# The begin of the second MLP product: three steps put in another order

## The chip, the cores and the metric

The kernel runs on one core of a Trainium2 chip. TensorE (PE in the profile) multiplies, VectorE (DVE), ScalarE (ACT) and GpSimd (POOL) work on elements, and SyncE (SP) issues the transfers between the chip's memory and the core. Each engine has a queue of its own and takes its instructions in the order in which the program gave them; engines wait for each other through semaphores. The metric is the device time of one execution in microseconds (us), lower is better.

## The reference

The kernel computes one layer of an encoder on 1024 tokens of width 1024, in float32. The part that matters here is the last line, the MLP:

```python
h = rms_norm(x, norm2_g[l]) @ w_mlp_in[l]          # 1024 x 4096
x = x + jnp.square(jax.nn.relu(h)) @ w_mlp_out[l]  # 4096 x 1024
```

Before it come a combined input projection, neighbourhood attention, a short gated convolution and the merge of both branches.

## The kernel before

Every float32 operand is scaled by a power of two and split into two float16 parts, a high part (written by ScalarE, `A.activation`) and a low part (the rest, written by VectorE, `V.scalar_tensor_tensor`). A product is three matmuls: high by high, high by low, low by high (`PASSES`).

Both MLP products save multiplications by working on 2 x 2 blocks with seven products in place of eight. Sums of blocks take the place of the eighth product.

*First MLP product.* It runs in 16 groups of columns (`quad(q)`, L1284). A group has seven banks of twelve matmuls. The first bank's result is copied by ScalarE (L1307); the others are added by VectorE straight out of PSUM into the group's tile `as` (the sums `post5`, `post7`, `post3` and two lambdas, L1295 to L1310). When a group's last sum is given out, a generator `h_done(q)` (L1267) is started. It makes relu on ScalarE (L1269), the square with its row sums (L1271), then four sums of blocks on POOL (`sums`, L1134, its instructions at L1138), and then one store of all seven forms to the chip's memory (`HS`, L1275).

*Second MLP product.* It runs over four slices `s` of the 4096, and in each over seven operands, in the order of `ORDER` (L1345): w11, t2, w21, t3, t1, t4, w22. An operand holds one form of h and one form of the weights, each with high and low part (tile `ops`). TensorE takes four banks of twelve matmuls for an operand (loop at L1479). `prep2(s)` (L1347) prepares the operands of a slice:

- it squares the weights on ScalarE (L1362, L1365) and has VectorE add the squares up (L924, L925). A small matmul (L179, on TensorE's own queue) sums over the partitions, and VectorE makes the slice's scale of that;
- POOL makes the weight form T2 (L1371, L1372);
- then for each operand it asks for the h of a later one (`h_load(n + 3)`, L1343, on SP's queue), lets ScalarE write the high part of h (L1397), VectorE the low part of h (L1399), ScalarE the high part of the weights in two halves (L1402) and VectorE the low part in two halves (L1406);
- behind some operands POOL makes the next weight forms in place: after w11 it adds w12 to w11 (L1411, two adds of 128 x 1024), after t2 it adds w22 to w12 (L1415), after t3 it completes T2 (L1419).

Operand 1 (t2 of slice 0) has a peculiarity: its h was loaded into the place where its weights' high part will be (L1377, L1378), so ScalarE's L1402 waits for VectorE's L1399.

*The order.* Nothing schedules itself. The program is written by generators: `fg` holds those that end the work of a group, `bg` those that prepare what comes. `unit` (L185) gives out the matmuls of a bank and then takes some steps of `fg` (`step`) and `bg` (`tick`). So the place of a `yield` decides where an instruction stands in its engine's queue. `need(i)` (L1182) ticks and steps until operand `i` has been given out in full; `gate(i)` keeps a generator back until TensorE's work that used the same place has been given out (`pe_done`). After group 15 the program loads the h of operands 2, 3 and 4, calls `settle()`, which gives out the sums that wait for their bank, and steps until no group is alive:

```python
    settle()
    while live:
        step()
```

Seen queue by queue, the kernel before has, around the change: VectorE has operand 0's low parts, operand 1's low parts, and among and behind these the last five sums of group 15. ScalarE has operand 0's and operand 1's high parts, then group 15's relu. POOL has group 14's four sums, the four adds L1411 and L1415, and then group 15's four sums. SP has group 14's store, the h of operands 2, 3 and 4, then group 15's store, the h of operands 5, 6 and 7, and the weights of slice 1.

Of the kernel before, what the change touches and what calls it, by code (L numbers as in the profile page):

```python
# [15 lines left out]
OP = mybir.AluOpType  # L16
# [36 lines left out]
def encoder_block(ctx: ExitStack, tc: tile.TileContext, x, weights, cols, gqk, rel, masks, out):  # L53
    nc = tc.nc
    V, A, G, T, SP = nc.vector, nc.scalar, nc.gpsimd, nc.tensor, nc.sync
# [27 lines left out]
    def cols_of(kind, n):  # L83
        a = area[kind]
        if a[1] + n > a[2]:
            assert kind != "keep"
            a[1] = a[0]
        a[1] += n
        return slice(a[1] - n, a[1])

    def keep(n=1):
        return cols_of("keep", n)
# [4 lines left out]
    def at(c, i, n=1):  # L97
        return slice(c.start + i, c.start + i + n)

    def mul(a, b, out=None):  # L100
        out = out or tmp(a.stop - a.start)
        V.tensor_tensor(sc[:, out], sc[:, a], sc[:, b], op=OP.mult)
        return out
# [23 lines left out]
    def step(n=1):  # L127
        for _ in range(n):
            for g in list(fg):
                if not advance(g):  # L130
                    fg.remove(g)

    def tick(n=1):

        for _ in range(n):
            i = 0
            while i < len(bg):
                r = advance(bg[i])
                if not r:
                    bg.pop(i)  # L140
                elif r == WAIT and side[0]:
                    i += 1
                else:
                    break
# [55 lines left out]
    def settle():  # L200
        while late:
            late.pop(0)()
# [9 lines left out]
    def load_upto(n):  # L212
        while loaded[0] < min(n, len(loads)):
            ch, p = loads[loaded[0]]
            loaded[0] += 1
            t = rawp.tile([128, 1024], F32, name="raw")
            load_into(t[:, :ch.widths[p][0] * ch.widths[p][1]], ch, p)
            ch.raw.append(t)
# [702 lines left out]
    def sum_of(sm):  # L921

        b, a = cols_of("prep", 1), ones_col()
        V.tensor_reduce(sc[:, b], sc[:, sm], axis=AX, op=OP.add)  # L924
        V.tensor_copy(a, sc[:, b])  # L925
        return a, work[0]

    def scale_of(am, more, n=3):

        a, mark = am  # L930
        yield from apart(mark, n * 6144, work)
        b, s, inv = cols_of("prep", 1), cols_of("prep", 1), keep()
        yield from all_sum(a, b, anybank(), 1e-36)
        yield from pow2_half(b, 14, s, inv, more)
        return s, inv
# [238 lines left out]
    pe_done, ready = [-2], set()  # L1174
# [3 lines left out]
    def gate(i):  # L1178
        while pe_done[0] < i - 2 or (i == 2 and pair_done[0] < 4):
            yield  # L1180

    def need(i):  # L1182
        while i not in ready:
            assert bg
            forced[0] = True
            tick()
            step()
        forced[0] = False
# [145 lines left out]
    def w2x_load(s):  # L1334
        pool = later["pool"] if s == 1 else wsp
        X2[s] = pool.tile([128, 4, 1024], F32, name="w2x", tag="w2x" if s == 1 else "ws", bufs=1 if s == 1 else 2)
        for i in range(4):
            load_into(X2[s][:, i], c2x[s], i)

    def h_load(n):  # L1340
        s, f = n // 7, ORDER[n % 7][0]
        later["h", n] = later["hf"][:, n % 4]
        SP.dma_start(later["h", n], HS[s][:, f])  # L1343
# [3 lines left out]
    def prep2(s):  # L1347
        raw, x2 = c2[s].raw, X2[s]
        w11, w12 = raw[0:2], raw[2:4]
        w21, w22 = [x2[:, i] for i in range(2)], [x2[:, i] for i in range(2, 4)]  # L1350
        while not r_ready[s]:
            yield
        Rs, iR = R[s]
        sm = cols_of("prep", 6)
        if s == 0:
            yield from gate(16)
            OPS[16] = TAGS[16 % 3][0].tile([128, 2, 2, 2048], F16, name="ops", tag=TAGS[16 % 3][1])
            j = OPS[16][:, 0, 0].bitcast(BF16)
        else:
            j = later["junk"]  # L1360
        for i in range(4):
            A.activation(j[:, :1024], raw[i], AF.Square, scale=sc[:, iR], accum_out=sc[:, at(sm, i)])  # L1362
            yield
        for i in range(2):
            A.activation(j, x2[:, 2 * i:2 * i + 2].rearrange("p a c -> p (a c)"), AF.Square, scale=sc[:, iR],  # L1365
                         accum_out=sc[:, at(sm, 4 + i)])
            yield
        sums = sum_of(sm)
        T2 = later["t2"]()
        for i in range(2):  # L1370
            G.tensor_tensor(T2[:, i], w12[i], w22[i], op=OP.add)  # L1371
            G.tensor_tensor(T2[:, i], T2[:, i], w11[i], op=OP.add)  # L1372
        yield
        if s == 0:
            yield from gate(17)
            P = OPS[17] = TAGS[17 % 3][0].tile([128, 2, 2, 2048], F16, name="ops", tag=TAGS[17 % 3][1])
            later["h", 1] = P[:, 0].rearrange("p w m -> p (w m)").bitcast(F32).rearrange("p (k t) -> p k t", k=4)  # L1377
            SP.dma_start(later["h", 1], HS[0][:, ORDER[1][0]])  # L1378
        sw, inv = yield from scale_of(sums, 0)
        fw = keep()  # L1380
        mul(iR, sw, fw)
        c2[s].inv = inv
        yield
        for o, (f, name) in enumerate(ORDER):
            n = 7 * s + o
            i = 16 + n
            yield from gate(i)
            pool, tag = TAGS[i % 3]
            if n > 1:
                OPS[i] = pool.tile([128, 2, 2, 2048], F16, name="ops", tag=tag)  # L1390
            P = OPS[i]
            while ("h", n) not in later:
                yield
            if 1 < n < 25:
                h_load(n + 3)
            hf = later.pop(("h", n)).rearrange("p k t -> p (k t)")
            A.activation(P[:, 1, 0], hf, AF.Copy, scale=sc[:, Rs])  # L1397
            yield
            V.scalar_tensor_tensor(P[:, 1, 1], hf, sc[:, Rs], P[:, 1, 0], op0=OP.mult, op1=OP.subtract)  # L1399
            w = {"w11": w11, "t1": w11, "t3": w12, "w21": w21, "w22": w22}.get(name) or [T2[:, i] for i in range(2)]  # L1400
            for i2 in range(2):
                A.activation(P[:, 0, 0, 1024 * i2:1024 * i2 + 1024], w[i2], AF.Copy, scale=sc[:, fw])  # L1402
            yield
            for i2 in range(2):
                sl = slice(1024 * i2, 1024 * i2 + 1024)
                V.scalar_tensor_tensor(P[:, 0, 1, sl], w[i2], sc[:, fw], P[:, 0, 0, sl], op0=OP.mult, op1=OP.subtract)  # L1406
                yield
            ready.add(i)
            if name == "w11":
                for i2 in range(2):  # L1410
                    G.tensor_tensor(w11[i2], w11[i2], w12[i2], op=OP.add)  # L1411
                yield
            elif name == "t2":
                for i2 in range(2):
                    G.tensor_tensor(w12[i2], w12[i2], w22[i2], op=OP.add)  # L1415
                yield
            elif name == "t3":
                for i2 in range(2):
                    G.tensor_tensor(T2[:, i2], T2[:, i2], w21[i2], op=OP.add)  # L1419
                yield  # L1420
            elif name == "t1":
                done[0] += 4
                load_upto(done[0] + 5)
                if s < 3:
                    w2x_load(s + 1)
                    bg.append(prep2(s + 1))
            yield
# [8 lines left out]

    bg.append(first2())
    bg.append(prep2(0))
    whole(14)
    whole(15)  # L1440
# [3 lines left out]
    for n in (2, 3, 4):  # L1444
        h_load(n)
    settle()
    while live:
        step()
    p4.close()
# [3 lines left out]
    t2 = w5p.tile([128, 2, 1024], F32, name="t2")  # L1453
# [119 lines left out]
```

## Time and profile before

| | |
|---|---|
| median of 3 runs | 1279.17 us (1278.58 to 1280.23) |
| the profiled execution | 1279.16 us, its span 1277.0 us |
| mean granted clock of TensorE | 0.985 |
| busy: TensorE, its weight loads | 1214.9 us (95%), 578.5 us (45%) |
| busy: VectorE, ScalarE, POOL | 961.3 us (75%), 763.7 us (60%), 463.0 us (36%) |
| share of TensorE in the chain that ended last | 66% |
| second MLP product | from 975.5 us to the end |

A row of a timeline reads: start, duration, engine, line of the kernel, operation, output tile and input tiles, shapes, how many instructions it merges, and in brackets how long the engine stood idle before it and what ended that. Times are us from the span's start. Matmul ends are modelled: one of 512 columns shows 0.379 us, while the next starts 0.216 us after it at full clock. The row of a tile gives the least, the median and the largest duration in ns, then the first and last start.

### The profile page before, as it was taken

To read this page: it belongs to the slowest core of one execution; us is meant where nothing else is said; L and a number is where in the kernel's file an instruction comes from. 1 tells how busy PE (TensorE), PEld (TensorE's weight loads), DVE (VectorE), ACT (ScalarE), POOL (GpSimd) and SP (SyncE) were. 2 spreads that over 40 slices of the span, in tenths; PEclk is the share of its full clock that TensorE was granted. 3 is DMA by queue.
4 is the path that set the end of the run, shared out by engine and by line. 5 is a ranking of instruction groups with operands and counts; after the bars stand their busy time and mean duration, and the time that the engine had idled before them with its cause. 6 is when DMAs were issued, how large, how long until landed. Compare 5 with 4: busy or idle time off the path is not lost.

```text
span 1277.0 us, 17035 instructions
## 1 busy us (share of the span) xinstructions
PE 1214.9 (95%) x6294; PEld 578.5 (45%) x6294; DVE 961.3 (75%) x1719; ACT 763.7 (60%) x1169; POOL 463.0 (36%) x277
## 2 busy tenths in 40 slices
PE   4999998998999999999997999999998999999998
PEld 3544444444444444444445644444443444444444
DVE  6668767878656876876576467766767889999997
ACT  6777567677564544533575777787774873646440
POOL 2430001211222111100112467866669455463462
PEclk9999998999999999999998999999999999999999
DMA  6558446556543212215277344534457553526212
GB/s 250 115 195 178 86 85 132 105 106 134 116 112 100 66 34 66 60 40 198 66 150 146 115 162 178 176 129 157 173 205 264 217 203 132 198 100 247 95 37 99
DMA packets 170803, 173.35 MB, mean 136 GB/s; under 512 B 131424, under 2 KB 131936, under 8 KB 166624
## 3 DMA queue, kind: packets, MB, share of 16 engines
q1 hardware_dynamic: 170720, 172.27, 45.5%
q8 instruction: 49, 0.80, 0.3%
q14 instruction: 34, 0.28, 0.1%
HBM read 102.51 MB, written 37.75 MB: 110 GB/s over the span
## 4 chain that ended last, share of the span: by engine, by line
PE 66%; DVE 15%; ACT 8%; DMA 5%; issue 4%; POOL 2%; SPq 1%; DVEq 0%; ACTq 0%; POOLq 0%
PE ps_d L188 24%; PE ps_s L188 22%; PE ps_o L188 14%; PE ps_d L854 5%; DMA PT<-P 2%; DMA hs<-as 2%; DVE w_s L971 1%; DVE w_ws L278 1%; ACT w L977 1%; POOL sform L480 1%; PE ps_s L778 1%; PE ps_o L835 1%; DVE sz L792 1%; DVE sc L301 1%; ACT raw L944 1%
## 5 line engine op out<-in xcount | busy, mean ns | idle before, releaser
L188 PEld LDWEIGHTS <-w 128*128 128x128 f16 x1512 | 148.2, 99 | 161.3 <-issue 11.0
L188 PEld LDWEIGHTS <-ops 128*128 128x128 f16 x1356 | 133.1, 98 | 164.1 <-issue 8.5
L1138 POOL TENSOR_TENSOR as<-as 128x512 f32<-128x512 f32 x64 | 110.8, 1731 | 69.0 <-ACT as L1271 65.3
L854 PE MATMUL ps_d<-uT,w_ws 128*128 128x512 f16 x528 | 129.7, 387 | 2.5 <-ACT w_ws L290 2.4
L188 PE MATMUL ps_d<-ops 128*128 128x512 f16 x492 | 115.4, 385 | 4.3 <-DVE as L1298 4.3
L188 PE MATMUL ps_s<-ops 128*128 128x512 f16 (+1 forms) x528 | 118.7, 375 | 0.0
L1397 ACT ACTIVATE ops<-hf,sc 128x2048 f16<-128x2048 f32 x26 | 52.0, 1999 | 95.1 <-PE ps_d L188 39.9
L188 PEld LDWEIGHTS <-uT 128*128 128x128 f16 x648 | 64.7, 100 | 70.5 <-issue 6.7
L971 DVE SCALAR_TENSOR_TENSOR w<-raw,sc,w 128x512 f16<-128x512 f32 (+1 forms) x32 | 40.7, 1271 | 67.8 <-ACT w L977 67.8
L188 PE MATMUL ps_d<-u2T,w 128*128 128x512 f16 (+1 forms) x420 | 89.0, 363 | 1.9 <-DMA u2T<-v 1.9
L188 PEld LDWEIGHTS <-w_s 128*128 128x128 f16 x588 | 57.1, 98 | 73.2 <-DMA uT<-gs 2.9
L188 PE MATMUL ps_s<-u2x,w 128*128 128x512 f16 (+1 forms) x396 | 83.3, 360 | 4.2 <-ACT v L1163 2.1
L944 ACT ACTIVATE raw<-raw,sc 128x256 f32<-128x256 f32 x184 | 76.0, 495 | 6.7 <-DVE w_ws L278 3.4
L958 POOL TENSOR_TENSOR tsum<-raw 128x512 f32<-128x512 f32 x30 | 50.8, 1707 | 79.7 <-ACT raw L944 66.5
L854 PEld LDWEIGHTS <-w_ws 128*128 128x128 f16 x528 | 51.6, 99 | 59.7 <-issue 5.6
L1399 DVE SCALAR_TENSOR_TENSOR ops<-hf,sc,ops 128x2048 f16<-128x2048 f32 x26 | 72.3, 2781 | 7.3 <-ACT ops L1397 7.3
L188 PE MATMUL ps_o<-ops 128*128 128x512 f16 x336 | 77.1, 379 | 0.0
L1269 ACT ACTIVATE as<-as 128x2048 f32<-128x2048 f32 x16 | 30.6, 1910 | 65.2 <-DVE as L1303 65.2
L958 POOL TENSOR_TENSOR gsum<-raw 128x512 f32<-128x512 f32 x14 | 18.5, 1340 | 135.6 <-issue 68.6
L971 DVE SCALAR_TENSOR_TENSOR w<-tsum,sc,w 128x1024 f16<-128x1024 f32 x30 | 61.5, 2088 | 0.0
L278 DVE SCALAR_TENSOR_TENSOR w_ws<-raw,sc,w_ws 128x512 f16<-128x512 f32 (+2 forms) x72 | 51.1, 764 | 3.5 <-ACT w_ws L290 3.5
L290 ACT ACTIVATE w_ws<-raw,sc 128x512 f16<-128x512 f32 (+2 forms) x72 | 40.9, 636 | 20.0 <-DVE sc L253 20.0
(302 smaller groups left out, 2558.5 us busy)
## 6 DMA issues: line engine op xcount, KB each, us to landing
raw<-in_weights SPq DMA_DIRECT2D x92, 512.0 KB, 4.1
hs<-as SPq DMA_DIRECT2D x16, 1792.0 KB, 6.9
hf<-hs SPq DMA_DIRECT2D x26, 1024.0 KB, 6.3
w2x<-in_weights SPq DMA_DIRECT2D x16, 512.0 KB, 7.4
raw<-in_weights SPq DMA_DIRECT2D x16, 384.0 KB, 3.8
xt<-in_x SPq DMA_DIRECT2D x8, 512.0 KB, 9.9
gs<-s SPq DMA_DIRECT2D x4, 1024.0 KB, 7.0
x<-in_x SPq DMA_DIRECT2D x8, 512.0 KB, 8.3
```

Source lines behind the costliest of these rows:

```text
L188: T.matmul(ps, l, r, start=a, stop=b)
L278: V.scalar_tensor_tensor(lo, self.raw[p][:, o:o + m], sc[:, c:c + 1], hi, op0=OP.mult, op1=OP.subtract)
L290: A.activation(self.parts[:, 0, f + o:f + o + m], self.raw[p][:, o:o + m], AF.Copy, scale=sc[:, c:c + 1])
L301: V.tensor_reduce(sc[:, at(rm, o, k)], self.raw[p][:, :k * w].rearrange("p (k w) -> p k w", k=k), axis=AX, op=OP.max, apply_absolute_value ...
L854: T.matmul(ps, l, r, start=a, stop=b)
L944: A.activation(v, v, AF.Copy, scale=sc[:, at(g, 4 * i + k)])
L958: G.tensor_tensor(t[:, o], a, b, op=OP.add)
L971: V.scalar_tensor_tensor(P[:, a:b, 1], w, sc[:, s], P[:, a:b, 0], op0=OP.mult, op1=OP.subtract)
L1138: sub.tensor_tensor(z[o], z[a], z[b], op=op)
L1269: A.activation(f[:, 0:4], f[:, 0:4], AF.Relu)
L1397: A.activation(P[:, 1, 0], hf, AF.Copy, scale=sc[:, Rs])
L1399: V.scalar_tensor_tensor(P[:, 1, 1], hf, sc[:, Rs], P[:, 1, 0], op0=OP.mult, op1=OP.subtract)
```

## The change

```diff
@@ prep2, for each operand n
             A.activation(P[:, 1, 0], hf, AF.Copy, scale=sc[:, Rs])
             yield
+            while n == 1 and pe_done[0] < 16:
+                yield
             V.scalar_tensor_tensor(P[:, 1, 1], hf, sc[:, Rs], P[:, 1, 0], op0=OP.mult, op1=OP.subtract)
...
             ready.add(i)
-            if name == "w11":
-                for i2 in range(2):
-                    G.tensor_tensor(w11[i2], w11[i2], w12[i2], op=OP.add)
-                yield
-            elif name == "t2":
-                for i2 in range(2):
-                    G.tensor_tensor(w12[i2], w12[i2], w22[i2], op=OP.add)
+            if name == "t2":
+                for a, b in ((w11, w12), (w12, w22)):
+                    for i2 in range(2):
+                        G.tensor_tensor(a[i2], a[i2], b[i2], op=OP.add)
                 yield
...
@@ after whole(15) and the loads of operands 2, 3 and 4
     settle()
+    need(17)
     while live:
         step()
```

It has three parts. The generator that prepares operand 1 stops ahead of the low part of h (L1399 before, L1401 after) until all matmuls of group 15 have been given out. The two adds to w11 move from behind operand 0 to behind operand 1, in front of the two adds to w12; this holds for all four slices. And after `settle()` the program gives out the rest of operand 1 before it steps on.

The number of instructions on every engine stays the same. In the built program the queues of slice 0 become: VectorE has operand 0's low parts, the last five sums of group 15, then operand 1's low parts, then operand 2's. ScalarE keeps its order. POOL has group 14's four sums, the first sum of group 15, the four adds, and then the other three sums of group 15. SP keeps its order. TensorE keeps its order.

## The prediction

> **What bounds the kernel now.** I read four views in this order: the busy times by stretch, TensorE's timeline where the first MLP product gives way to the second, the timelines of the other engines there, and the transfers behind. By stretch:
>
> ```profile
> 975.50:1277.00 301.50, 293.44 (x1360) 133.29 (x1358) 277.66 (x248) 145.91 (x131) 153.88 (x52) 0.99 0.43 157
> ```
>
> The columns are the stretch, its length, then the busy us of TensorE, its weight loads, VectorE, ScalarE and POOL, then the granted clock. The second product is TensorE's: 293.44 of 301.50 us. What is missing lies at its begin (twelve matmuls fill one bank):
>
> ```profile
> 975.49 2.75 PE L188 MATMUL ps_o<-ops 128*128 128x512 f16 x12
> 978.08 2.75 PE L188 MATMUL ps_d<-ops 128*128 128x512 f16 x12
> 980.67 2.75 PE L188 MATMUL ps_s<-ops 128*128 128x512 f16 x12
> 987.75 5.28 PE L188 MATMUL ps_d<-ops 128*128 128x512 f16 x12 [4.32 <-DVE as L1298]
> 992.82 3.21 PE L188 MATMUL ps_s<-ops 128*128 128x512 f16 x12
> 995.87 2.75 PE L188 MATMUL ps_o<-ops 128*128 128x512 f16 x12
> ```
>
> Banks follow each other every 2.59 us (975.49, 978.08, 980.67). Operand 0's fourth bank should start at 983.26 and starts at 987.75; it and a part of the next run slowly. The bank of 995.87 would have stood at 975.49 + 5 × 2.59 = 988.44, so the whole loss is 7.43 us. That is all this place can give. The slow part is the clock (stretch, length, TensorE's busy us, granted clock):
>
> ```profile
> 983.42:987.75 4.33, 0.01 (x2) 0.90 1.00 416
> 987.75:993.90 6.15, 6.15 (x15) 0.51 0.17 71
> ...
> 733.50:737.90 4.40, 1.65 (x8) 0.98 0.94 324
> 737.90:741.20 3.30, 3.29 (x9) 0.51 0.68 265
> ```
>
> After an idle stretch of 4.33 us TensorE is granted 0.51 of its clock for 6.15 us; after one of 2.75 us (4.40 − 1.65) for 3.30 us. Half the clock loses half of that: 1.65 to 3.1 us.
>
> VectorE holds the bank up:
>
> ```profile
> 970.41 2.34 DVE L1399 SCALAR_TENSOR_TENSOR ops<-h,sc,ops 128x2048 f16<-128x2048 f32 x1
> ...
> 976.09 4.43 DVE L1399 SCALAR_TENSOR_TENSOR ops<-ops,sc 128x2048 f16<-128x2048 f32 x1
> 981.79 2.02 DVE L1406 SCALAR_TENSOR_TENSOR ops<-h,sc,ops 128x1024 f16<-128x1024 f32 x1 [1.28 <-ACT ops L1402]
> ...
> 984.34 2.76 DVE L1406 SCALAR_TENSOR_TENSOR ops<-h,sc,ops 128x1024 f16<-128x1024 f32 x1
> 987.02 0.68 DVE L1298 TENSOR_TENSOR as<-ps_d,as 128x512 f32<-128x512 f32 x1
> ...
> 988.93 0.68 DVE L1303 TENSOR_TENSOR as<-ps_s,as 128x512 f32<-128x512 f32 x1
> ```
>
> ```profile
> 975.05 7.68 POOL L1411 TENSOR_TENSOR raw<-raw 128x1024 f32<-128x1024 f32 x2 [1.17 <-DVE ops L1406]
> ```
>
> ```profile
> L1371 POOL TENSOR_TENSOR h<-raw,w2x x2: 2352/2360/2367, 956.1 to 960.9; 128x1024 f32<-128x1024 f32 x2
> ```
>
> ```profile
> L1138 POOL TENSOR_TENSOR as<-as x64: 1261/1600/3331, 715.4 to 999.7; 128x512 f32<-128x512 f32 x64
> ```
>
> ```profile
> L1406 DVE SCALAR_TENSOR_TENSOR ops<-raw,sc,ops x24: 1271/1273/3378, 972.7 to 1236.0; 128x1024 f16<-128x1024 f32 x24
> ```
>
> Group 15's sums (L1298 to L1303) stand behind operand 1's low parts. These are slow because POOL runs: 4.43 us beside it against 2.34 without, the halves 2.02 and 2.76 against 1.27; and two of POOL's adds take 7.68 us where one takes 2.36 alone (a sum of a group, L1138, at least 1.26). 4.43 is 2.34 and the rest of an add: the two engines take turns, an instruction at a time. Sums out of PSUM keep their 0.68.
>
> **The change part by part.** No instruction is added or removed; the order alone changes.
>
> *Sums ahead of operand 1's low parts.* VectorE has done operand 0's halves at 976.1. Five sums, 0.6 to 0.7 apart (L1310, L1298 to L1303), end at 979.2, and the one that frees the bank (L1300) at 978.7, before 983.26. The wait and its clock drop go: 7.43 us. TensorE now wants operand 1 at 975.49 + 4 × 2.59 = 985.85.
>
> *The adds leave POOL.* From 974 on POOL is idle, so operand 1's low part of h takes 2.34 (979.2 to 981.5). ScalarE's high parts of its weights wait for that, as before:
>
> ```profile
> 980.61 2.19 ACT L1402 ACTIVATE ops<-h,sc 128x1024 f16<-128x1024 f32 x2 [6.01 <-DVE ops L1399]
> 989.65 1.91 ACT L1269 ACTIVATE as<-as 128x2048 f32<-128x2048 f32 x1 [6.85 <-DVE as L1303]
> ...
> 993.50 0.19 ACT L1271 ACTIVATION_READ_ACCUMULATOR as<-as,sc 128x1 f32 x1
> ```
>
> They run from 981.6 to 983.8, and with two halves at 1.27 operand 1 is complete at 985.3, in time by half a microsecond; a miss costs TensorE that much.
>
> *Relu behind operand 1.* It starts at 983.8 instead of 989.65 and ends, as the row of 993.50 does 4.04 after it, at 987.8. ScalarE's high part of operand 2's h then ends at 989.7.
>
> *What POOL does next.* In the built order POOL has group 15's first sum, the four adds, the other three sums and the store. That first sum waits for the relu, and the adds behind it: they start at 989.1, just ahead of operand 2's low parts at 989.7. With the lengths alone, less a tenth that neighbours overlap (2.3 an add, 1.2 a sum, 2.2 and 1.1 VectorE's 2048 and 1024 columns), the turns are: add to 991.4, operand 2's low h 993.6, add 995.8, first half 996.9, add 999.1, second half 1000.2, add 1002.4, operand 3's low h 1004.6, sum 1005.8, half 1006.9, sum 1008.0, half 1009.1, sum 1010.3. TensorE wants operand 2 at 985.85 + 10.36 = 996.2. Its second matmul waits for the first half (0.5), its eighth for the second (2.0): 2.6 us, for now. Operand 2 ends at 1009.1, when operand 3 is ready.
>
> *What is late next.* Group 15's store goes at 1010.3 instead of 1001.90, and on SP's queue stand behind it the h of operands 5, 6 and 7 and the next weights:
>
> ```profile
> 1001.90 0.53 SPq L1275 DMA_DIRECT2D hs<-as  x1
> 1002.48 5.20 SPq L1343 DMA_DIRECT2D hf<-hs  x3
> ```
>
> ```profile
> L1343 SPq DMA_DIRECT2D hf<-hs x1: 654/654/654, 1002.5 to 1002.5; - x1
> ...
> DMA to landing us min/median/max: 10.6/10.6/10.6
> ```
>
> ```profile
> 997.56 0.67 ACT L1493 ACTIVATE acc<-ps_o,sc 128x512 f32<-128x512 f32 x1
> 998.13 0.67 ACT L1493 ACTIVATE acc<-ps_d,sc 128x512 f32<-128x512 f32 x1
> ...
> 1014.20 2.00 ACT L1397 ACTIVATE ops<-hf,sc 128x2048 f16<-128x2048 f32 x1 [4.01 <-PE ps_d L188]
> 1016.11 2.17 ACT L1402 ACTIVATE ops<-h,sc 128x1024 f16<-128x1024 f32 x2
> 1018.19 0.67 ACT L1493 ACTIVATE acc<-ps_s,sc 128x512 f32<-128x512 f32 x1
> ...
> 1025.14 1.99 ACT L1397 ACTIVATE ops<-hf,sc 128x2048 f16<-128x2048 f32 x1
> ```
>
> ```profile
> 1038.87 0.16 DVE L925 CAST ones<-sc 128x1 bf16<-128x1 f32 x1
> ```
>
> ```profile
> 1039.89 0.17 PE L179 MATMUL ps_d<-ones 128*128 128x1 bf16 x1
> ```
>
> Operand 5's h landed at 1002.48 + 10.6 = 1013.1, and ScalarE took it at 1014.20: 1.1 us of slack. Now it lands at 1010.3 + 0.6 + 10.6 = 1021.5. Behind the waiting L1397 stand, in ScalarE's order, operand 5's weights, four evictions (L1493), operand 6, and all the squares of the next weights (L1362, L1365). VectorE adds these up (L925), and TensorE's own queue holds the small matmul L179 on that sum. L179 came 0.86 us after its input: no room there either.
>
> From operand 5's h to that input: 4.0 us to the first eviction (1014.20 to 1018.19), 2.3 for four at 0.57 apart (997.56, 998.13), then 1025.14 to 1039.03, 13.9: together 20.2. It is ready at 1021.5 + 20.2 = 1041.7. TensorE gets there at 1039.89 − 7.43 + 2.6 = 1035.1, or 1035.4 with a short wait for VectorE's eviction of operand 2's first bank. It waits 6.3 us, and L179 runs at 1041.7, 1.8 us later than before. Whatever was won or lost earlier drops out.
>
> A wait of 6.3 us is longer than the two above, so the clock drops again: 1.65 to 3.1 us. I take the middle, 2.4; the two rows show both lengths and nothing says which.
>
> The Trainium skill ("TensorE: Matmul & The Clock Gate", "The HAM clock gate") says the clock halves after an idle window of about 3.4 us and returns after a busy one, with windows that run free. By it, one to two windows at half clock cost 1.7 to 3.4 us and the sum would be 1282.7 to 1284.4 (an estimate); the rows' 3.30 and 6.15 us agree.
>
> Behind L179 operand 7 needs some 12 us on VectorE and ScalarE, and TensorE has six banks (15.5 us) until then: nothing more is lost.
>
> **Sum.** The profiled execution took 1279.16 us (span 1277.0); the median is 1279.17. 1279.16 + 1.8 + 2.4 = 1283.4. With the store a microsecond off either way (about one turn) this case alone holds 1281.6 to 1285.1.
>
> **The rivals.** *Faster: the store is not late.* If POOL's eight instructions ran at their length alone from 987.8, the store would go at 987.8 + 4 × 1.3 + 4 × 2.36 = 1002.4, operand 5's h land at 1013.6, L179's input be ready at 1033.8, before TensorE: 1279.16 − 7.43 + 2.9 = 1274.6. It decides for a store before about 1006: L179 would be 31.4 later, at 1037.4, and a drop of 2.4 bring it back to 1039.9. For it: POOL is idle until 987.8. Against it: the 7.68 for two adds, with six of VectorE's low parts in the same stretch.
>
> The Trainium skill ("SBUF — State Buffer", "Who interferes with whom") makes it a lock: a VectorE instruction with two SBUF inputs and a GpSimd one that reads SBUF exclude each other for a whole instruction. The rows of 4.43 and 0.68 agree, and by it the sum stays 1283.4.
>
> *No measurable change.* The store goes at 1008.5, L179 falls where it was, and the drop is the small one: 1279.16 + 1.65 = 1280.8. Or the change doesn't do what it says: the stall goes from the bank to operand 2's low parts, with L179 in time, and two drops leave 1279.16 − 7.43 + 2.9 + 2 × 2.4 = 1279.4. For it: terms of a few microseconds that nearly cancel. Against it: 1.8 us of turns would have to go.
>
> *Slower still.* The store takes longer, as an earlier one did (13.5 us against 8.9 for that of 1001.90):
>
> ```profile
> L1275 SPq DMA_DIRECT2D hs<-as x1: 525/525/525, 953.2 to 953.2; - x1
> ...
> DMA to landing us min/median/max: 8.0/10.8/13.5
> ```
>
> ```profile
> L1275 SPq DMA_DIRECT2D hs<-as x1: 525/525/525, 1001.9 to 1001.9; - x1
> ...
> DMA to landing us min/median/max: 8.9/8.9/8.9
> ```
>
> That is 4.6 us more for operand 5's h: 1288.0. Against it: the queue is empty at 1010, as at 1001.90.
>
> **How the numbers follow.** Forecast 0.68, slower still 0.05, no measurable change 0.14, faster 0.13. So slower by over 0.2% (2.6 us, about what a measurement here can tell) 0.73, within it 0.14, faster 0.13. The range leaves out the faster case and the worst: 1277.5 to 1285.5.
>
> **What would show it.** In the changed kernel: no idle before operand 0's fourth bank, operand 1 at 985.9; the adds on POOL from 989 on at 3 us and more each; operand 2 beginning with two short waits, 2 to 3 us together; group 15's store at 1010 ± 1; ScalarE idle until about 1021.5 for a transfer; TensorE idle 5 to 7 us before L179 at 1041.7, and half its clock for 3 to 6 us behind it. I am wrong if the store goes before 1006, if operand 5's h lands in less than 8 us, or if L179's wait costs no clock.

## The result, and the profile after

The changed kernel takes 1282.07 us (median of 16 runs, 1280.29 to 1287.28) beside 1279.04 us for the kernel before (16 runs on the same chip). The ratio is 1.0028, with a 95% interval of 1.0017 to 1.0038: slower by 3.6 us (2.2 to 4.9); the two medians lie 3.0 us apart. The forecast was 1283.4 us and a loss of 4.2 us.

The profiled execution of the changed kernel took 1282.2 us (span 1280.1 us), that of before 1279.16 us (span 1277.0 us). The stages ahead of the second MLP product differ between executions by some microseconds, of one kernel too: operand 0's first bank began at 977.01 and at 981.09 us in two executions of the last experiment's kernel. So I compare from the start of operand 0's first bank to the end of the span. The first row is from before, in the view by stretch; the columns are those of the prediction:

```profile
975.49:1277.00 301.51, 293.45 (x1360) 133.30 (x1358) 277.67 (x248) 145.91 (x131) 153.89 (x52) 0.99 0.43 157
1039.89:1277.00 237.11, 233.37 (x1096) 106.83 (x1094) 223.59 (x208) 102.01 (x87) 113.07 (x39) 1.00 0.35 127
```

The same view of the changed kernel:

```profile
975.51:1280.10 304.59, 292.85 (x1360) 132.76 (x1358) 279.05 (x248) 145.68 (x131) 150.69 (x52) 0.99 0.42 155
1041.26:1280.10 238.84, 235.07 (x1095) 107.14 (x1095) 225.91 (x209) 103.05 (x87) 114.92 (x40) 0.99 0.35 128
```

The second product is 3.08 us longer. The second rows begin at L179, so they divide this: 1.35 us are lost up to L179 (65.75 against 64.40 us) and 1.73 us behind it. TensorE's timeline of the changed kernel shows where:

```profile
983.28 2.75 PE L188 MATMUL ps_d<-ops 128*128 128x512 f16 x12
985.87 2.75 PE L188 MATMUL ps_s<-ops 128*128 128x512 f16 x12
...
996.23 0.38 PE L188 MATMUL ps_o<-ops 128*128 128x512 f16 x1
996.92 1.46 PE L188 MATMUL ps_o<-ops 128*128 128x512 f16 x6 [0.31 <-DVE ops L1408]
1000.20 1.24 PE L188 MATMUL ps_o<-ops 128*128 128x512 f16 x5 [1.83 <-DVE ops L1408]
1001.27 2.75 PE L188 MATMUL ps_d<-ops 128*128 128x512 f16 x12
...
1025.97 2.75 PE L188 MATMUL ps_s<-ops 128*128 128x512 f16 x12 [1.05 <-ACT acc L1493]
...
1033.74 2.75 PE L188 MATMUL ps_o<-ops 128*128 128x512 f16 x12
1041.26 0.18 PE L179 MATMUL ps_d<-ones 128*128 128x1 bf16 x1 [4.77 <-DVE ones L925]
1041.30 4.44 PE L188 MATMUL ps_s<-ops 128*128 128x512 f16 x12
```

The stall of before at operand 0's fourth bank is gone (983.28, no idle ahead of it), and operand 1 begins at 985.87. Then come four new losses, each against banks 2.59 us apart: 2.45 us at operand 2 (1001.27 − 996.23 − 2.59), 1.39 us at operand 4 (1.21 of it ahead of 1025.97), 4.93 us ahead of L179 (1041.26 − 1033.74 − 2.59), and the 1.73 us behind L179, where the first bank takes 4.44 us and 2.75 is usual. Together they cost 10.50 us, against the 7.43 us that are won: 3.07. The last of the four is the clock; in the stretch behind L179 the granted clock (third column from the end) is 0.61:

```profile
1041.44:1045.74 4.30, 4.30 (x13) 1.56 (x12) 4.20 (x10) 1.27 (x1) 3.15 (x2) 0.61 0.30 120
```

POOL's timeline of the changed kernel:

```profile
987.82 1.27 POOL L1138 TENSOR_TENSOR as<-as 128x512 f32<-128x512 f32 x1 [13.94 <-ACT as L1271]
989.05 6.73 POOL L1414 TENSOR_TENSOR raw<-raw 128x1024 f32<-128x1024 f32 x2
995.75 6.60 POOL L1414 TENSOR_TENSOR raw<-raw,w2x 128x1024 f32<-128x1024 f32 x2
1002.32 7.74 POOL L1138 TENSOR_TENSOR as<-as 128x512 f32<-128x512 f32 x3
```

POOL stands idle for 13.94 us until the relu and the square behind it (L1271) are done, makes group 15's first sum, and then the four adds stand ahead of the other three sums. They take 13.3 us, beside operand 2's low parts. From there the chain that ended last (start, length, what) leads through the store to L179:

```profile
989.09 13.26 POOL raw L1414 x4
...
1010.08 0.53 SPq L1275
1010.65 10.52 DMA hf<-hs
1021.27 2.00 ACT ops L1397
...
1041.26 0.18 PE ps_d L179
```

### The profile page after: what moved, and what is told of

Its sections match the earlier page's. It is cut to its first block, busy times and chain, and to the rows that moved or that the text cites. A ratio compares the mean times of both kernels' runs of the same rounds, so it can differ in the third digit from the quotient of the medians.

```text
span 1280.1 us, 17037 instructions
## 1 busy us (share of the span) xinstructions
PE 1210.4 (95%) x6294; PEld 577.0 (45%) x6294; DVE 962.1 (75%) x1719; ACT 763.2 (60%) x1169; POOL 459.4 (36%) x277
## 4 chain that ended last, share of the span: by engine, by line
PE 62%; DVE 15%; ACT 9%; DMA 5%; issue 4%; POOL 3%; SPq 1%; DVEq 0%; ACTq 0%; POOLq 0%
PE ps_d L188 22%; PE ps_s L188 20%; PE ps_o L188 13%; PE ps_d L854 4%; DMA hs<-as 2%; DMA PT<-P 1%; DVE w_s L971 1%; ACT w L977 1%; POOL as L1138 1%; POOL raw L1414 1%; DVE w_ws L278 1%; POOL sform L480 1%; DVE sz L792 1%; DVE P L818 1%; DMA hf<-hs 1%
## 5 line engine op out<-in xcount | busy, mean ns | idle before, releaser
L1401 DVE SCALAR_TENSOR_TENSOR ops<-hf,sc,ops 128x2048 f16<-128x2048 f32 x26 | 76.1, 2926 | 8.0 <-ACT ops L1397 8.0
```

## The experiments

All times are medians beside runs of the kernel before on the same chip; the ratio is to these. "Second product" is the stretch from operand 0's first bank to the end of the span, as above. All experiments keep the amount of work, but for 21 matmuls more in "TensorE kept busy". The row of "adds divided" is the second of its two measurements.

| kernel | median us | ratio (95%) | group 15's store, from operand 0's start | wait ahead of L179 | second product |
|---|---|---|---|---|---|
| before | 1279.04 to 1279.98 | 1 | 26.41 | none | 301.51 |
| after | 1282.07 | 1.0028 (1.0017 to 1.0038) | 34.57 | 4.77 | 304.59 |
| after, once more | 1283.83 | 1.0025 (1.0016 to 1.0034) | 34.85 | 4.76 | 305.23 |
| first and third part | 1276.88 | 0.9983 (0.9971 to 0.9995) | 29.78 | 0.38 | 298.23 |
| second part | 1280.9 | 1.0004 (0.9995 to 1.0014) | 27.00 | none | 301.86 |
| adds behind the sums | 1277.65 | 0.999 (0.9977 to 1.0003) | 20.47 | none | 299.51 |
| without the third part | 1277.05 | 0.9982 (0.9971 to 0.9992) | 16.43 | none | 300.91 |
| operand 5's h early | 1277.15 | 0.9981 (0.9968 to 0.9995) | 35.94 | 1.57 | 299.86 |
| TensorE kept busy | 1281.52 | 1.0017 (1.0003 to 1.0031) | 35.02 | 0.23 | 303.63 |
| adds divided | 1273.19 | 0.9947 (0.9933 to 0.996) | 22.07 | none | 295.69 |

**First and third part alone.** The adds stay where the kernel before has them: to w11 behind operand 0, to w12 behind operand 1.

```diff
--- after
-            if name == "t2":
-                for a, b in ((w11, w12), (w12, w22)):
-                    for i2 in range(2):
-                        G.tensor_tensor(a[i2], a[i2], b[i2], op=OP.add)
+            if name == "w11":
+                for i2 in range(2):
+                    G.tensor_tensor(w11[i2], w11[i2], w12[i2], op=OP.add)
+                yield
+            elif name == "t2":
+                for i2 in range(2):
+                    G.tensor_tensor(w12[i2], w12[i2], w22[i2], op=OP.add)
```

> The kernel before, with the first and the third part of the change alone: group 15's sums ahead of operand 1's low parts, the adds to w11 and to w12 where they were. Theory by turns: two adds run from 976 to 980.7 while VectorE adds out of PSUM, operand 1 is complete at 986.6, still in time; relu ends at 989.1; first sum of group 15 to 990.4, two adds and three sums take turns with operand 2's and 3's low parts, the store goes at 1005.0 instead of 1010.1. Operand 5's h lands at 1016.1, L179's input is ready at 1036.2; TensorE waits 2.7 us at operand 2 and comes to L179 at 1035.2 to 1036.9. Time 1275.7 (1275 to 1277): about 3 us faster than before. Rival (the moved sums alone cost the time, by whatever they delay): slower than before.

Measured: 1276.88 us, 0.9983 (0.9971 to 0.9995): faster than before. POOL's timeline, then TensorE's:

```profile
973.98 5.65 POOL L1413 TENSOR_TENSOR raw<-raw 128x1024 f32<-128x1024 f32 x2 [1.16 <-DVE ops L1408]
988.07 1.27 POOL L1138 TENSOR_TENSOR as<-as 128x512 f32<-128x512 f32 x1 [8.44 <-ACT as L1271]
989.30 6.71 POOL L1417 TENSOR_TENSOR raw<-raw,w2x 128x1024 f32<-128x1024 f32 x2
```

```profile
997.15 1.45 PE L188 MATMUL ps_o<-ops 128*128 128x512 f16 x6 [2.08 <-DVE sc L112]
999.36 1.24 PE L188 MATMUL ps_o<-ops 128*128 128x512 f16 x5 [0.76 <-DVE ops L1408]
...
1034.65 0.18 PE L179 MATMUL ps_d<-ones 128*128 128x1 bf16 x1 [0.38 <-DVE ones L925]
```

With two adds instead of four between the relu's first sum and the others, group 15's store goes at 1003.75 (4.8 us earlier, counted from operand 0's start), and L179's wait shrinks from 4.77 to 0.38 us, with no slow bank behind it. L179 comes 30.90 us after the store, against 31.18 in the changed kernel: the same chain, and here it just fails to matter. So the first and the third part together are a gain, and the loss needs the second part.

**Second part alone.** In the kernel before, only the adds to w11 move behind operand 1.

```diff
--- before
-            if name == "w11":
-                for i2 in range(2):
-                    G.tensor_tensor(w11[i2], w11[i2], w12[i2], op=OP.add)
-                yield
-            elif name == "t2":
-                for i2 in range(2):
-                    G.tensor_tensor(w12[i2], w12[i2], w22[i2], op=OP.add)
+            if name == "t2":
+                for a, b in ((w11, w12), (w12, w22)):
+                    for i2 in range(2):
+                        G.tensor_tensor(a[i2], a[i2], b[i2], op=OP.add)
```

> The kernel before with the second part of the change alone: the adds to w11 move behind operand 1, the rest of the order stays. My theory: the order on POOL stays what it was (four adds, then group 15's four sums), since group 15's first sum is given out behind the adds there; the adds start some microseconds later or at the same time, the store of group 15 at 1001.9 to 1004, the wait of 4.3 us at operand 0's fourth bank stays, L179 does not wait or by less than 1 us: 1279.7 us (1278.5 to 1281). The rival, that the moved adds by themselves make the store late, expects the store at 1008 or later, a wait at L179 and 1282 us or more.

Measured: 1280.9 us, 1.0004 (0.9995 to 1.0014): no change that can be told. Its POOL timeline:

```profile
973.29 7.68 POOL L1412 TENSOR_TENSOR raw<-raw 128x1024 f32<-128x1024 f32 x2 [1.16 <-DVE ops L1406]
980.94 6.61 POOL L1412 TENSOR_TENSOR raw<-raw,w2x 128x1024 f32<-128x1024 f32 x2
992.61 8.10 POOL L1138 TENSOR_TENSOR as<-as 128x512 f32<-128x512 f32 x4 [5.06 <-ACT as L1271]
```

The adds keep their place ahead of group 15's sums, because in this program they are given out before the relu. The stall at operand 0's fourth bank stays, with a wait of 4.92 us. The loss comes when the relu's first sum is given out ahead of the adds, so that they wait for it, while the other sums wait for them.

**Adds behind the sums.** The changed kernel, with all four adds held back until group 15 is done.

```diff
--- after
             if name == "t2":
+                while s == 0 and live:
+                    yield
```

> The changed kernel, with the four adds held back until all four sums of group 15 have been given out, so that the store is not behind them. Theory: store at about 996 instead of 1010.1, operand 5's h at 1007, no wait for it at L179; but the adds to w12 end at 1008.3 instead of 1002.3, and operand 3, which needs them, is late: TensorE waits 4.8 us in three pieces at operand 3 and loses 1.7 to 3 us of clock. Time 1278.5 (1277 to 1280): the place of the wait moves, 3 to 4 us under the changed kernel. Rival (operand 2's wait is the cost): with operand 2 no longer waiting, and if operand 3 is in time after all, 1274.

Measured: 1277.65 us, 0.999 (0.9977 to 1.0003). TensorE's timeline, then ScalarE's:

```profile
1010.98 2.18 PE L188 MATMUL ps_s<-ops 128*128 128x512 f16 x7 [3.25 <-ACT acc L1495]
1013.61 2.12 PE L188 MATMUL ps_s<-ops 128*128 128x512 f16 x5 [0.45 <-DVE ops L1408]
...
1038.87 0.17 PE L179 MATMUL ps_d<-ones 128*128 128x1 bf16 x1
```

```profile
1006.91 1.15 ACT L1404 ACTIVATE ops<-raw,sc 128x1024 f16<-128x1024 f32 x1 [10.01 <-POOL raw L1416]
...
1010.26 0.67 ACT L1495 ACTIVATE acc<-ps_s,sc 128x512 f32<-128x512 f32 x1
```

The store goes 14.1 us earlier than in the changed kernel, and the wait at L179 is gone. In its place operand 3 is late: its weights need the adds to w12, ScalarE waits 10.01 us for them, and operand 1's evictions (L1495) stand behind that, so TensorE waits 3.25 us for a bank and 0.45 us inside it. The clock drops here too: the twelve matmuls of this bank show 2.18 and 2.12 us where seven and five show 1.67 and 1.24 at full clock, 1.39 us more. That is less than the 1.7 to 3 us expected. L179's wait thus hangs on the time of the store, and the adds can be too late as well as too early.

**Without the third part.** The changed kernel without `need(17)`.

```diff
--- after
     settle()
-    need(17)
     while live:
```

> The kernel after without its third part (operand 1 is not given out in full before the program steps on). Group 15's relu then stands ahead of operand 1's weights on ScalarE and all four of its sums ahead of the four adds on POOL; operand 1's low parts stand on VectorE behind group 15's row sums. My theory: the store of group 15 goes at about 990, operand 5's h lands before 1002, L179 does not wait; in exchange operand 1 is late: its low part of h runs from 983.5 beside POOL's sums, its first half is ready at about 989.5, and TensorE waits some 3.7 us at 985.85 and loses 1.65 us of clock: 1279.04 - 7.43 + 3.7 + 1.65 = 1277.0 us (1275.5 to 1279). The rival, that the third part has no share in the loss, expects the time of the changed kernel, 1282, with a wait of 4 us and more at L179.

Measured: 1277.05 us, 0.9982 (0.9971 to 0.9992). TensorE's timeline, then two stretches of it (TensorE's busy time is the third column, the granted clock the third from the end):

```profile
988.52 0.38 PE L188 MATMUL ps_s<-ops 128*128 128x512 f16 x1 [2.50 <-ACT ops L1404]
990.82 3.97 PE L188 MATMUL ps_s<-ops 128*128 128x512 f16 x11 [1.93 <-DVE ops L1408]
...
1039.32 0.17 PE L179 MATMUL ps_d<-ones 128*128 128x1 bf16 x1
```

```profile
988.52:990.82 2.30, 0.38 (x1) 0.09 (x1) 2.30 (x2) 2.30 (x3) 2.22 (x2) 0.90 0.33 139
990.82:993.80 2.98, 2.98 (x8) 1.05 (x8) 2.95 (x4) 2.98 (x3) 2.98 (x2) 0.51 0.24 89
```

The relu then runs before operand 1, all four sums stand ahead of the adds, and the store goes at 991.92. L179 waits for nothing. The price is operand 1, late by 2.50 and 1.93 us, and a stretch at half clock. So the loss needs the third part as well as the second: with either of them left out, the kernel is no slower than before. The second and third without the first weren't tried, nor the first or the third alone, so whether the loss needs the first part too stays open.

**Operand 5's h early.** In the changed kernel the load that waits behind group 15's store on SP's queue is issued with those of operands 2 to 4, ahead of that store. The weights of the next slice stay behind it.

```diff
--- after
-            if 1 < n < 25:
+            if 2 < n < 25:
                 h_load(n + 3)
...
-    for n in (2, 3, 4):
+    for n in (2, 3, 4, 5):
         h_load(n)
```

> The changed kernel, with the load of operand 5's h given out beside those of operands 2, 3 and 4, so ahead of group 15's store on SP's queue; nothing else moves. Theory (the late store holds up operand 5's h, ScalarE behind it, and by the squares' sum the small matmul L179): operand 5's h lands at about 993 instead of 1021.2; operand 6's h, now first behind the store, at 1021.2, some 6.3 us earlier in ScalarE's order than the step it held before; then the last of the next weights bind, so L179 runs at about 1036.9 instead of 1041.3, TensorE waits under 2 us there and keeps its clock. Time 1276.0 (1275 to 1278), 6 us under the changed kernel. Rival (what costs is that operand 2's low parts wait for POOL's adds, 2.4 us, and what TensorE loses behind it): nothing there is changed, 1282 (within 1).

Measured: 1277.15 us, 0.9981 (0.9968 to 0.9995). SP's timeline, then TensorE's, then ScalarE's:

```profile
976.82 4.30 SPq L1343 DMA_DIRECT2D hf<-hs  x4
1011.18 0.53 SPq L1275 DMA_DIRECT2D hs<-as  x1
```

```profile
998.01 1.46 PE L188 MATMUL ps_o<-ops 128*128 128x512 f16 x6 [1.11 <-DVE ops L1408]
1001.30 1.24 PE L188 MATMUL ps_o<-ops 128*128 128x512 f16 x5 [1.83 <-DVE ops L1408]
...
1037.96 0.18 PE L179 MATMUL ps_d<-ones 128*128 128x1 bf16 x1 [1.57 <-DVE ones L925]
```

```profile
1035.42 2.00 ACT L1365 ACTIVATE junk<-w2x,sc 128x2048 bf16<-128x2048 f32 x1 [0.44 <-DMA w2x<-in_weights]
```

The store goes 1.4 us later than in the changed kernel (35.94 against 34.57 us), and the waits at operand 2 stay, yet 4.7 us of the second product are gone: 304.59 − 299.86. This is the direct test of the path from the store over operand 5's h to L179. What is left of L179's wait, 1.57 us, has another releaser: the next slice's weights, still behind the store, for which the last two squares wait (1.61 and 0.44 us). The expected gain was somewhat larger, because I had put L179 some 1.3 us earlier, counted from operand 0's start.

**TensorE kept busy.** In the changed kernel 21 matmuls of 512 columns run right ahead of L179, in the bank that L179 then overwrites. They add work, but only in time in which TensorE waits.

```diff
--- after
+    dummy = []
 ...
+        if dummy:
+            P, n = dummy.pop()
+            for i in range(n):
+                T.matmul(bk, P[:, 1, 0, :128], P[:, 0, 0, :512], start=i == 0, stop=i == n - 1)
 ...
+        dummy[:] = [(P, 21)] if n == 5 else []
```

> The changed kernel, with 21 matmuls more of 512 columns (4.5 us) in TensorE's queue right ahead of L179, into the bank that L179 then overwrites; they only fill TensorE's wait of 4.77 us. Theory: L179 stays at 1041.3, as its input sets it; TensorE was not idle, so its clock stays full behind it, and the drop's price falls away: 1282.1 - 1.7 = 1280.4. A theory without a price for the clock: 1282.1. A theory by which TensorE itself was late at L179: the 4.5 us come on top, 1286.6.

Measured: 1281.52 us, 1.0017 (1.0003 to 1.0031). TensorE's timeline (L185 is L179 of the others), and the stretch from it to the end:

```profile
1034.11 4.70 PE L184 MATMUL ps_d<-ops 128*128 128x512 f16 x21
1039.04 0.16 PE L185 MATMUL ps_d<-ones 128*128 128x1 bf16 x1 [0.23 <-DVE ones L931]
1039.07 2.75 PE L194 MATMUL ps_s<-ops 128*128 128x512 f16 x12
```

```profile
1039.04:1276.20 237.16, 233.37 (x1095) 106.77 (x1094) 223.89 (x209) 103.05 (x87) 116.37 (x40) 1.00 0.36 129
```

The small matmul comes no earlier than in the changed kernel (66.47 us from operand 0's start, against 65.75), but the bank behind it takes 2.75 us, and from there to the end pass 237.16 us: the 237.11 of before, not the 238.84 of the changed kernel. So the second half of the loss, 1.68 us, is the clock after an idle wait. The changed order of the adds holds for the other three slices too; since the stretch from L179 on is as long as before, it costs nothing there. The whole time, 1281.52 us, lies between the 1280.4 of the theory and the 1282.1 without a price for the clock, and the intervals of the ratios of this kernel and the changed one overlap; by the whole times alone it is not settled which holds, and the traces settle it.

**The changed kernel once more**, beside the second part alone, the kernel without the third part and the next one.

> The changed kernel itself, beside the others on one chip: 1282.1 us (1281 to 1283.5), the store of group 15 at 1010.1, the wait at L179 4.8 us. If the half-clocked stretch behind L179 depends on where the idle time falls, its length may be another than the 1.7 us lost before (up to 3.1 us): then the time is up to 1.4 us longer.

Measured: 1283.83 us, 1.0025 (1.0016 to 1.0034). L179 in TensorE's timeline, and the stretch from it to the end:

```profile
1041.16 0.19 PE L179 MATMUL ps_d<-ones 128*128 128x1 bf16 x1 [4.76 <-DVE ones L925]
```

```profile
1041.16:1280.50 239.34, 235.59 (x1095) 107.40 (x1095) 226.00 (x209) 103.05 (x87) 114.64 (x40) 0.99 0.36 128
```

The same wait (4.76 against 4.77 us) costs 2.23 us of clock this time (239.34 − 237.11), where it cost 1.73 before. The median lies above the 1281 to 1283.5 us expected and within the 1.4 us more that were allowed for a longer half-clocked stretch; the one profile shows 0.5 us of that.

**Adds divided.** The kernel before with the first and the third part; the adds to w11 stay behind operand 0, while POOL is idle anyway, and the adds to w12 are held back behind all of group 15's sums.

```diff
--- before
             yield
+            while n == 1 and pe_done[0] < 16:
+                yield
             V.scalar_tensor_tensor(P[:, 1, 1], hf, sc[:, Rs], P[:, 1, 0], op0=OP.mult, op1=OP.subtract)
...
             elif name == "t2":
+                while s == 0 and live:
+                    yield
                 for i2 in range(2):
                     G.tensor_tensor(w12[i2], w12[i2], w22[i2], op=OP.add)
...
     settle()
+    need(17)
```

> The kernel before with the first and the third part of the change, the two adds to w11 where they were (behind operand 0, while POOL is idle), and the two adds to w12 held back behind all four of group 15's sums. My theory: what the change costs is only that the adds stand between group 15's first sum and its others; with two of them done before the relu ends and two behind the sums, the store of group 15 goes at about 997.5, operand 5's h lands at about 1008.6, L179 does not wait. TensorE waits some 0.75 us at operand 2 and as much at operand 3, without a loss of clock: 1279.04 - 7.43 + 1.5 = 1273.1 us (1272 to 1275), faster than both kernels. The rival, that the moved low parts and not the adds' place make the loss (collisions of VectorE and POOL anywhere), expects the waits at operands 2 and 3 to grow to 4 us and more, a drop of the clock with it, and 1277 us or more.

> The same kernel once more, for a second measurement of its time and a profile of an execution near its median. My theory: 1273 us (1272 to 1274.5), 7 us under the kernel before beside it; waits of about 0.95 us at operand 2 and 0.4 us at operand 3, no half-clocked stretch between operand 0 and the next weights' L179. The rival, that the first 1273.06 was the chip's luck (its profiled execution took 1279.5), expects 1276 us or more.

Measured: 1273.06 us, ratio 0.9951 (0.9933 to 0.9969), and the second time 1273.19 us, 0.9947 (0.9933 to 0.996): 6.8 us faster than before (5.1 to 8.6), and faster than the changed kernel by more than either interval. The first profiled execution took 1279.54 us, 4.7 us more than the second one; 4.1 us of that lie ahead of the second product (operand 0 began at 981.09, against 977.01), which itself took 296.31 us. I show the second one, POOL and then TensorE:

```profile
976.86 5.64 POOL L1413 TENSOR_TENSOR raw<-raw 128x1024 f32<-128x1024 f32 x2 [1.16 <-DVE ops L1408]
990.94 8.12 POOL L1138 TENSOR_TENSOR as<-as 128x512 f32<-128x512 f32 x4 [8.44 <-ACT as L1271]
```

```profile
1000.19 1.24 PE L188 MATMUL ps_o<-ops 128*128 128x512 f16 x5 [0.76 <-DVE ops L1408]
...
1011.14 1.24 PE L188 MATMUL ps_s<-ops 128*128 128x512 f16 x5 [0.43 <-DVE ops L1408]
...
1035.53 0.17 PE L179 MATMUL ps_d<-ones 128*128 128x1 bf16 x1
```

Two adds run in what was POOL's idle time, all four sums follow the relu at once, and the store goes at 999.08, which is 12.5 us earlier than in the changed kernel (from operand 0's start). The stall, L179's wait and the half clock are all gone (the granted clock is 1.00 over the second product); what stays are two short waits. The stretch of 295.69 us is 5.82 us shorter than that of before, of the 7.43 that the prediction called all that this place can give.

## Why the prediction was right

The forecast held in its sign and its mechanism, and nearly in its size: a loss of 4.2 us was forecast, the ratio gives 3.6 (2.2 to 4.9) and the profiled second product 3.08. By its own steps:

- *The stall and its half clock go, 7.43 us.* Right. Operand 0's fourth bank began at 983.28 with no idle ahead of it, operand 1 at 985.87 (985.85 forecast). The last experiment shows that 5.82 of the 7.43 us can be kept.
- *Operand 1 in time by half a microsecond, relu done at 987.8.* Right: TensorE waits for nothing at operand 1, and POOL's first sum begins at 987.82 on the relu's end.
- *POOL and VectorE take turns behind it.* Right, turn by turn: the adds from 989.05 (989.1) to 1002.35 (1002.4), the waits at operand 2 end at 996.92 and 1000.20 (996.9 and 1000.2), the store goes at 1010.08 (1010.3).
- *Operand 5's h, and L179 behind it.* Right in the path, which the early load shows by cutting it. ScalarE took operand 5's h at 1021.27 (1021.5), and L179 ran at 1041.26 (1041.7), 1.35 us later than before where 1.8 was forecast. The terms of this sum were each a few tenths too long: the store 0.2 us, its landing 0.1, the way from there to L179 0.2.
- *TensorE waits 6.3 us there.* Too long: 4.77 us by the list, 4.93 from when the next matmul was due, and so just short of the 5 to 7 us that were to show it. The step that was missed is that TensorE's third bank of operand 4 waits for the eviction of operand 3's first, which ScalarE has queued behind its wait for operand 5's h (1.05 us at 1025.97). I had allowed for 0.3 us, for VectorE's eviction. It cost nothing, since it only took time from the wait for the same transfer.
- *The clock drops again, 2.4 us.* The term that was mis-sized: 1.73 us in the first profile and 2.23 in the second. It lies within the bounds that I gave, 1.65 to 3.1, and the middle was a choice between two rows: that the second profile comes close to it is luck. With 1.35 + 1.73 the profiled sum is 3.08 instead of 4.2.

Of the rivals, *the store is not late* fell by the store's time. The "adds divided" kernel, whose store goes earlier still (22.07 us from operand 0's start), shows what an early store gives: 1273.2 us, where the rival said 1274.6. Its point of decision, a store before about 1006, agrees with the first experiment: there the store goes 29.78 us from operand 0's start, which is 1005.3 on the clock of the trace before, L179 waits only 0.38 us, and the kernel is faster than before. *No measurable change* needed a store at 1008.5, and it went at 1010.08. *The stall goes to operand 2 with L179 in time* describes the "first and third part" kernel, but for the clock: its waits of 2.08 and 0.76 us cost none. The *slower store* didn't happen: the store landed 8.9 us after its issue and operand 5's h 10.5 us after its own, as before.

The prediction cited the Trainium skill ("SBUF — State Buffer", "Who interferes with whom") for a lock between VectorE with two SBUF inputs and GpSimd. The runs agree: two adds take 7.68 us beside low parts out of SBUF ("second part"), and 5.65 us where sums out of PSUM run beside most of them ("first and third part").

## What to carry to other kernels

When work is moved out of an engine's busy stretch, ask what its new place is queued between: here four adds came to stand between the first and the last of a group's sums, and a store, a load, ScalarE's queue and a small matmul on TensorE's own queue all hung on the last. Follow the queue past the wait that you remove, to the next thing that has no slack, and count the slack there (1.1 us here) before counting the gain. If idle time is what the moved work leaves behind (13.94 us on POOL), it is worth dividing the work: the half that has its inputs can stay.

## What the runs showed of the hardware

In these traces the price of an idle stretch in clock doesn't follow its length. I count the idle time from when the next matmul was due, and the price as what the start of the banks behind it lost beyond that time. In the kernel before 4.49 us of idle cost 2.94 us (7.43 − 4.49), the same stall of 5.09 us in "second part" cost 2.62, but 4.93 us ahead of L179 cost 1.73 in the changed kernel, and the same wait 2.23 in another execution. Two waits of 2.50 and 1.93 us with a single matmul between them took the clock to 0.51, and 3.25 and 0.45 us with seven between to 0.54. Behind 2.08 and 0.76 us, or 1.11 and 1.83 us, with six between, and behind a single wait of 1.57 us, the granted clock stayed at 1.00.

The Trainium skill ("TensorE: Matmul & The Clock Gate", "The HAM clock gate") says that activity is watched in windows of about 3.4 us that run free, so that the number of slow matmuls depends on where they fall. Two prices for one wait agree with that. The drop behind 2.50 and 1.93 us, with a matmul between, and the one behind 2.75 us in the prediction's rows show that here no unbroken idle of 3.4 us was needed. That is shorter than the idle window which the prediction cited from the same page of the Trainium skill, and there the trace decides.
